# Feed-forward tiles of a two-layer encoder: transposed by DMA in two 16-bit planes instead of on TensorE

## The chip, the cores and the metric

The kernel runs on one core of a Trainium2 chip. The metric is device time of one execution in microseconds. The kernel before was run three times: 2039.32, 2039.69 and 2040.37 us, median 2039.69.

## The reference

Two encoder layers work on 256 tokens of width 2048. Each layer mixes tokens, attends to 256 memory tokens, projects out, and ends in a gated feed-forward of width 5632:

```python
D_FF = ((8 * D_MODEL // 3 + 255) // 256) * 256

def swiglu(h, w_gate_up, w_down):
    gate, up = jnp.split(h @ w_gate_up, 2, axis=-1)
    return (jax.nn.silu(gate) * up) @ w_down

def reference(x, mem, ...):
    for l in range(DEPTH):
...
        x = x + jnp.concatenate([tok_out, mem_out], axis=-1) @ w_out[l]
        x = x + swiglu(rms_norm(x, g_ffn[l]), w_gate_up[l], w_down[l])
    return x
```

All data are float32.

## The kernel before

Every product is made from three products of parts: a matrix is split into a rounded part (`hi`, written as float32r by ScalarE) and the rest (`lo`, subtracted by VectorE), and TensorE multiplies hi by hi, lo by hi and hi by lo (lines 198 to 200 in `matmul3`). For weights the split is `halves` (L254 on ScalarE, L255 on VectorE); for activations it is `split` (L192, L193). SP loads the weights from HBM into `raw` tiles, of which there are four; the split weights `whi` and `wlo` have three buffers each, so ScalarE can run at most two buffers ahead of the one that TensorE reads.

The feed-forward of a layer runs over 11 feature blocks of 512 columns, in chunks of 4, 4 and 3 blocks. For each block a `Pair` multiplies the normalized input (`hF`) by the block's gate and up columns, in eight steps over the 2048 rows of the weights; a step loads a 256-row strip of both. Up to three of the eight steps ("fast") use sums of the operands to save one of eight products: VectorE makes the sums of the weights (L347 to L350, into `raw` and `T`), and both `raw` and `T` are split. The other steps split `raw` alone. Then ScalarE makes silu of the gate (L785), VectorE multiplies by up (L786) into a tile `sg` of 128 tokens by 512 features, one for each of the two row tiles t.

For the down projection the features must lie on the partitions, so `turn_a` transposes each `sg` tile: four TensorE transposes of 128x128 into a PSUM bank (L204, through `transpose4`), then `split` into hi and lo. For some blocks (`quick`) a copy of two of the four pieces (L773, 128x256) is kept in SBUF, from which `activation_sums` makes the sums that fast steps of the down projection need. `turn_a` is called with a delay by `later`: 12 steps after its block, or 3 steps for the last block of a chunk. After a chunk's blocks two Pairs of the down projection add the chunk's share to the residual X.

Calls of `later` and the order of statements give the order of the program; the tile framework's scheduler then interleaves the instructions of each engine. Each engine works through its queue in that fixed order and waits at an instruction whose operands are not there. Feed-forward tiles of 512 columns (`big`) come from a pool of 26 (`FFN_TILES`).

Of the kernel before, what the change touches and what calls it, by code (L numbers as in the profile page):

```python
# [9 lines left out]

F32 = mybir.dt.float32
F32R = mybir.dt.float32r
AF = mybir.ActivationFunctionType
ALU = mybir.AluOpType
AX = mybir.AxisListType

P = 128
# [36 lines left out]
def encoder(ctx: ExitStack, tc: tile.TileContext, x, mem, g_mix, g_ffn, w_in_a, g_v_a, w_spatial, b_spatial,  # L54
            w_in_b, g_q_b, g_k_b, g_mem, w_mem_kv, g_mq, g_mk, w_out, w_gate_up, w_down, rope_c, rope_s, out):
    nc = tc.nc
# [14 lines left out]
    def nm(s):  # L71
        uid[0] += 1
        return f"{s}_{uid[0]}"

    def big(dt=F32, shape=None):
        return room["p"].tile(shape or [P, NB], dt, tag="a", name=nm("a"))
# [4 lines left out]
    def misc():  # L81
        return psm.tile([P, NB], F32, tag="m", name=nm("m"))

    def v4(a):
        return a.rearrange("p (c n) -> p c n", n=P)
# [10 lines left out]
    def later(delay, fn):  # L96
        queue.append((clock[0] + delay, len(queue), fn))
# [24 lines left out]
    def load_x(t, j):  # L122
        nc.sync.dma_start(X[t][j], x[0, t * P:(t + 1) * P, j * NB:(j + 1) * NB])
# [3 lines left out]
    def load_gain(kind, g, tile):  # L127
        gst[kind] = tile
        nc.scalar.dma_start(gst[kind], g.rearrange("l (c p) -> (l c) p", p=P))
# [7 lines left out]
    def gslice(kind, l):  # L137
        return gcol[kind][:, 16 * l:16 * l + 16]

    load_gain("mix", g_mix, kp.tile([32, P], F32, tag="sg", name="gst_mix", bufs=2))  # L140
    nc.scalar.activation(junk[:, :8], mhalf, AF.Square)
    load_x(0, 0)
# [45 lines left out]
    def split(src, shape):  # L188

        hi = big(F32R, shape)  # L190
        lo = big(F32R, shape)
        nc.scalar.copy(hi, src)  # L192
        nc.vector.tensor_tensor(lo, src, hi.bitcast(F32), ALU.subtract)  # L193
        return hi, lo
# [7 lines left out]
    def transpose4(src, dst):  # L202
        for c in range(4):
            nc.tensor.transpose(dst[:, c * P:(c + 1) * P], src[:, c * P:(c + 1) * P], ident)  # L204

    def square_sum(src, out):
        for i in range(2):
            nc.scalar.activation(junk, src[:, 2 * P * i:2 * P * (i + 1)], AF.Square, accum_out=out[:, i:i + 1])

    def norm_piece(src, t, j, g, parts, keep):  # L210

        tp = misc()
        transpose4(src, tp)
        gained(tp, t, j, g, parts, keep)
        return tp
# [4 lines left out]
    def gained(tp, t, j, g, parts, keep):  # L220

        hi = keep(F32R, [P, 4, P])
        lo = keep(F32R, [P, 4, P])
        for c in range(4):
            gc = g[:, 4 * j + c:4 * j + c + 1]
            nc.scalar.activation(hi[:, c, :], v4(tp)[:, c, :], AF.Copy, scale=gc)
            nc.vector.scalar_tensor_tensor(lo[:, c, :], v4(tp)[:, c, :], gc, hi[:, c, :].bitcast(F32), ALU.mult,
# [20 lines left out]
    def halves(raw, n, step=KC4):  # L248

        hi = wp.tile([P, KC4, NB], F32R, tag="whi", name=nm("whi"))[:, :n]  # L250
        lo = wp.tile([P, KC4, NB], F32R, tag="wlo", name=nm("wlo"))[:, :n]
        for c in range(0, n, step):
# [47 lines left out]
    def activation_sums(a0, a1):  # L300

        q = big(F32, [P, 4, P])
        nc.vector.tensor_tensor(q[:, 0], a1[:, 0], a1[:, 1], ALU.subtract)
        nc.vector.tensor_tensor(q[:, 2], a1[:, 0], a0[:, 0], ALU.subtract)
        nc.vector.tensor_tensor(q[:, 1], a0[:, 0], q[:, 0], ALU.subtract)
        nc.vector.tensor_tensor(q[:, 3], a0[:, 1], q[:, 1], ALU.subtract)
        hi, lo = split(q, [P, 4, P])
        return [(hi[:, i, :], lo[:, i, :]) for i in range(4)]
# [106 lines left out]
    def head_norm(acc, r, gain, rope=False):  # L415

        ss = small(8)
        for t in range(NT):
            for h in range(4):
                hs = slice(h * P, (h + 1) * P)  # L420
                nc.scalar.activation(junk[:, :P], acc[t][:, hs], AF.Square, scale=r[t],
                                     accum_out=ss[:, 4 * t + h:4 * t + h + 1])
# [24 lines left out]
    def heads_T(qn):  # L447

        hi = [big(F32R, [P, 2, S]) for _ in range(2)]
        lo = [big(F32R, [P, 2, S]) for _ in range(2)]  # L450
        for t in range(NT):
            ts = slice(t * P, (t + 1) * P)
            tp = misc()
            transpose4(qn[t], tp)
            for pr in range(2):
                src = v4(tp)[:, 2 * pr:2 * pr + 2, :]
                nc.scalar.copy(hi[pr][:, :, ts], src)
                nc.vector.tensor_tensor(lo[pr][:, :, ts], src, hi[pr][:, :, ts].bitcast(F32), ALU.subtract)
        return hi, lo

    def attend(qn, waits, keys, values, kv_of, kc0, parts):
# [10 lines left out]
        def scores(pr):  # L472
            for h in (2 * pr, 2 * pr + 1):
# [10 lines left out]
                for t in range(NT):  # L484
                    nc.scalar.activation(pe[:, t * S:(t + 1) * S], sc[:, t * S:(t + 1) * S], AF.Exp,
                                         bias=nmx[:, t:t + 1], accum_out=sm[:, t:t + 1])
# [40 lines left out]
    def scaled(acc, r):  # L527

        res = []
        for t in range(NT):  # L530
            hi = big(F32R)
            lo = big(F32R)
            nc.scalar.activation(hi, acc[t], AF.Copy, scale=r[t])
            nc.vector.scalar_tensor_tensor(lo, acc[t], r[t], hi.bitcast(F32), ALU.mult, ALU.subtract)
# [64 lines left out]
    def residual_turns(j, norm, g, parts):  # L599
        add_residual(None, j, norm, g, parts)  # L600
# [4 lines left out]
    for l in range(DEPTH):  # L605
# [4 lines left out]
        if l == 0:  # L610
# [15 lines left out]
            def turn_spatial(i, a):  # L626
                tp = misc()
                transpose4(a, tp)
                wsT[i] = big()
                nc.scalar.copy(wsT[i], tp)  # L630
# [80 lines left out]
        else:  # L711
# [12 lines left out]
            for c in range(3):  # L724
                acc = linear(hT, w, c * NB)
                attend(head_norm(acc, norm.r, ghead["q"], True), (5, 6, 10, 13), lambda: own["k"], lambda: own["v"],
                       lambda h, c=c: (4 * c + h) // 3, 4 * c, cat)
# [32 lines left out]
        for chunk in (range(0, 4), range(4, 8), range(8, 11)):  # L760
            aT, aS, half = Parts(), {}, {}
            quick = [2 * f + 1 for f in chunk[:2 if chunk[-1] < 10 else l]]

            def turn_a(a, t, f, aT=aT, aS=aS, half=half, quick=quick):
                tp = misc()
                transpose4(a, tp)
                hi, lo = split(v4(tp), [P, 4, P])
                for i in range(4):
                    aT.put(4 * f + i, t, hi[:, i, :], lo[:, i, :])
                i = 2 * f + 1  # L770
                if i in quick:
                    half[i, t] = big(F32, [P, 2, P])
                    nc.scalar.copy(half[i, t], v4(tp)[:, 2:4])  # L773
                    if t == NT - 1:
                        aS[i] = activation_sums(half[i, 0], half[i, 1])

            pairs = {}
            for f in chunk:
                order, some = ((3, 4, 5, 0, 6, 1, 7, 2), 2) if f == 0 else ((0, 3, 1, 4, 2, 5, 6, 7), 3)
                pairs[f] = Pair(hF, sums, w_gate_up[l], f * NB, DFF + f * NB, order, fast[:some])  # L780
            for f, g in pairs.items():
                g.run(pairs.get(f + 1))
                for t in range(NT):
                    a = kp.tile([P, NB], F32, tag="sg", name=nm("sg"), bufs=2)
                    nc.scalar.activation(a, g.out[t][0], AF.Silu, scale=norm.r[t])  # L785
                    nc.vector.scalar_tensor_tensor(a, g.out[t][1], norm.r[t], a, ALU.mult, ALU.mult)  # L786
                    later(3 + t if f == chunk[-1] else 12 + t, lambda a=a, t=t, f=f: turn_a(a, t, f))
            last = chunk[-1] == 10
            every = [2 * f + c for f in chunk for c in range(2)]
            slow = [i for i in every if i not in quick]  # L790
            pairs = []
            for jj in range(2):
                order = list(slow)
                for n, i in enumerate(quick):
                    order.insert(2 * n + (0 if jj and not last else 2), i)
                into = [[X[t][2 * jj + n] for n in range(2)] for t in range(NT)]
                pairs.append(Pair(aT, aS, w_down[l], 2 * jj * NB, (2 * jj + 1) * NB, order, quick, into))
            for jj, g in enumerate(pairs):
                g.run(None if jj else pairs[1])
                for j in (2 * jj, 2 * jj + 1):  # L800
                    if last and l < DEPTH - 1:
                        residual_turns(j, next_norm, gslice("mix", l + 1), hT)
                    elif last:
                        for t in range(NT):
                            parts = 2 if j == 3 and t == NT - 1 else 1
                            for i in range(parts):
                                cs = slice(i * NB // parts, (i + 1) * NB // parts)
                                eng = nc.scalar if i else nc.sync
                                eng.dma_start(out[0, t * P:(t + 1) * P, j * NB + cs.start:j * NB + cs.stop],
                                              X[t][j][:, cs])  # L810
# [37 lines left out]
```

## Time and profile before

| | |
|---|---|
| median of three runs | 2039.69 us |
| profiled execution, first to last instruction (its span) | 2038.5 us |
| HBM traffic over the span | 194 GB/s |
| TensorE clock granted | 1.000 |
| tiles transposed in the feed-forwards | 44 (176 transposes) |

No separate time of the profiled execution is given beside its span. In the profile PE is TensorE's multiplication, PEld its weight load, DVE is VectorE, ACT ScalarE, POOL GpSimd, SP the engine that issues the weight loads; a q behind the name is an engine's queue of issued DMAs. A row of a group reads: line, engine, operation, output<-input, sizes, count, then busy time in us and mean ns of one, then idle time just before these instructions and what ended most of it. Busy times of one engine overlap somewhat, since instructions are pipelined.

### The profile page before, as it was taken

To read this page: it belongs to the slowest core of one execution; us is meant where nothing else is said; L and a number is where in the kernel's file an instruction comes from. 1 tells how busy PE (TensorE), PEld (TensorE's weight loads), DVE (VectorE), ACT (ScalarE), POOL (GpSimd) and SP (SyncE) were. 2 spreads that over 40 slices of the span, in tenths; PEclk is the share of its full clock that TensorE was granted. 3 is DMA by queue.
4 is the path that set the end of the run, shared out by engine and by line. 5 is a ranking of instruction groups with operands and counts; after the bars stand their busy time and mean duration, and the time that the engine had idled before them with its cause. 6 is when DMAs were issued, how large, how long until landed. Compare 5 with 4: busy or idle time off the path is not lost.

```text
span 2038.5 us, 24693 instructions
## 1 busy us (share of the span) xinstructions
PE 2027.7 (99%) x9298; PEld 1679.9 (82%) x9298; DVE 1605.0 (79%) x1862; ACT 1095.0 (54%) x1389; POOL 50.6 (2%) x80
## 2 busy tenths in 40 slices
PE   9999999999999999999999999999999999999999
PEld 7888888888888888888888888888888888888887
DVE  5675557998879988887566886589979899798876
ACT  7765455454445554444555765555544455444552
POOL 2010000000000000000010100000000000000000
PEclk9999999999999999999999999999999999999999
DMA  9754554646656465665566544555566555565554
GB/s 325 253 179 155 185 188 154 227 165 206 203 190 227 165 207 196 202 227 194 186 198 204 173 133 141 202 185 178 195 206 218 195 184 190 205 221 192 183 197 137
DMA packets 202432, 396.08 MB, mean 194 GB/s; under 512 B 11068, under 2 KB 11432, under 8 KB 202312
## 3 DMA queue, kind: packets, MB, share of 16 engines
q1 hardware_dynamic: 198800, 385.79, 56.6%
q0 software_dynamic: 2048, 6.42, 1.0%
q10 hardware_dynamic: 1464, 2.28, 0.3%
q8 instruction: 73, 1.20, 0.2%
q14 instruction: 47, 0.39, 0.1%
HBM read 390.26 MB, written 4.19 MB: 194 GB/s over the span
## 4 chain that ended last, share of the span: by engine, by line
PE 96%; DVE 3%; DMA 1%; issue 1%; ACT 0%; SPq 0%; DVEq 0%; ACTq 0%
PE acc L200 27%; PE acc L199 27%; PE acc L198 27%; PE m L200 4%; PE m L198 4%; PE m L199 4%; PE m L204 2%; DVE wlo L255 1%; DMA raw<-in_w_gate_up 1%; PE m L500 0%; PE m L643 0%; ACT whi L254 0%; DVE x L413 0%; DVE e L413 0%; DMA x<-in_x 0%
## 5 line engine op out<-in xcount | busy, mean ns | idle before, releaser
L254 ACT CAST whi<-raw 128x2048 fp32r<-128x2048 f32 (+2 forms) x465 | 700.8, 1539 | 585.0 <-PE acc L199 512.5
L255 DVE TENSOR_TENSOR wlo<-raw,whi 128x2048 fp32r<-128x2048 f32 (+2 forms) x465 | 836.4, 1823 | 223.9 <-ACT whi L254 220.1
L198 PE MATMUL acc<-whi,h 128*128 128x512 f32 x1440 | 563.7, 392 | 0.0
L199 PE MATMUL acc<-whi,h 128*128 128x512 f32 x1440 | 562.6, 391 | 0.0
L200 PE MATMUL acc<-wlo,h 128*128 128x512 f32 x1440 | 524.1, 392 | 0.9 <-DVE wlo L255 0.9
L198 PE MATMUL acc<-whi,a 128*128 128x512 f32 x1062 | 414.8, 391 | 0.0
L199 PE MATMUL acc<-whi,a 128*128 128x512 f32 x1062 | 414.2, 390 | 0.0
L200 PE MATMUL acc<-wlo,a 128*128 128x512 f32 x1062 | 398.2, 391 | 0.0
L200 PEld LDWEIGHTS acc<-wlo,h 128*128 128x128 f32 x1440 | 270.6, 188 | 56.6 <-DVE wlo L255 1.5
L199 PEld LDWEIGHTS acc<-whi,h 128*128 128x128 f32 x1440 | 270.7, 188 | 55.3
L198 PEld LDWEIGHTS acc<-whi,h 128*128 128x128 f32 x1440 | 271.0, 188 | 54.0
L200 PEld LDWEIGHTS acc<-wlo,a 128*128 128x128 f32 x1062 | 199.4, 188 | 41.3 <-DVE wlo L255 0.3
L199 PEld LDWEIGHTS acc<-whi,a 128*128 128x128 f32 x1062 | 199.5, 188 | 40.4
L198 PEld LDWEIGHTS acc<-whi,a 128*128 128x128 f32 x1062 | 199.5, 188 | 40.2
L254 ACT CAST whi<-T 128x1536 fp32r<-128x1536 f32 x82 | 121.4, 1480 | 143.8 <-PE acc L199 102.2
L255 DVE TENSOR_TENSOR wlo<-T,whi 128x1536 fp32r<-128x1536 f32 x82 | 143.5, 1750 | 39.1 <-ACT whi L254 39.0
L198 PE MATMUL m<-whi,a 128*128 128x512 f32 x264 | 104.2, 395 | 0.7 <-ACT whi L254 0.7
L199 PE MATMUL m<-whi,a 128*128 128x512 f32 x264 | 102.9, 390 | 0.0
L347 DVE TENSOR_TENSOR raw<-raw 128x512 f32<-128x512 f32 x82 | 56.1, 684 | 54.9 <-DMA raw<-in_w_gate_up 53.5
L200 PE MATMUL m<-wlo,a 128*128 128x512 f32 x264 | 89.6, 389 | 0.0
L192 ACT CAST a<-m 128x512 fp32r<-128x512 f32 x80 | 46.7, 587 | 42.8 <-PE m L204 31.7
L193 DVE TENSOR_TENSOR a<-m,a 128x512 fp32r<-128x512 f32 x80 | 53.8, 682 | 13.1 <-ACT a L192 12.9
(126 smaller groups left out, 1473.1 us busy)
## 6 DMA issues: line engine op xcount, KB each, us to landing
raw<-in_w_gate_up SPq DMA_DIRECT2D x352, 512.0 KB, 4.7
raw<-in_w_down SPq DMA_DIRECT2D x176, 512.0 KB, 5.2
raw<-in_w_out SPq DMA_DIRECT2D x32, 1024.0 KB, 5.1
raw<-in_w_in_a SPq DMA_DIRECT2D x24, 1024.0 KB, 5.2
raw<-in_w_in_b SPq DMA_DIRECT2D x24, 1024.0 KB, 5.1
raw<-in_w_mem_kv SPq DMA_DIRECT2D x16, 1024.0 KB, 5.1
raw<-in_w_in_a SPq DMA_DIRECT2D x7, 512.0 KB, 6.2
x<-in_x SPq DMA_DIRECT2D x8, 256.0 KB, 5.8
```

The lines of the kernel that those rows point to most:

```text
L192: nc.scalar.copy(hi, src)
L193: nc.vector.tensor_tensor(lo, src, hi.bitcast(F32), ALU.subtract)
L198: nc.tensor.matmul(out, lhsT=a[0], rhs=b[0], start=start, stop=False)
L199: nc.tensor.matmul(out, lhsT=a[1], rhs=b[0], start=False, stop=False)
L200: nc.tensor.matmul(out, lhsT=a[0], rhs=b[1], start=False, stop=stop)
L204: nc.tensor.transpose(dst[:, c * P:(c + 1) * P], src[:, c * P:(c + 1) * P], ident)
L254: nc.scalar.copy(hi[:, cut], raw[:, cut])
L255: nc.vector.tensor_tensor(lo[:, cut], raw[:, cut], hi[:, cut].bitcast(F32), ALU.subtract)
L347: nc.vector.tensor_tensor(raw[:, 0], raw[:, 0], raw[:, 1], ALU.add)
```

## The change

A new helper `turned` replaces the four TensorE transposes. It reads a tile of 128x512 float32 as 128x1024 16-bit words. ScalarE copies the words into two planes (all low halves, then all high halves); one DMA transpose of 16-bit words, issued from ScalarE's queue, turns the planes block by block into a second tile; a second ScalarE copy puts the halves together again in the first tile. The values are moved bit by bit, so the result is the same number for number. `turn_a` takes hi and lo from that tile, and the copy of two pieces now stands before the split.

```diff
+U16 = mybir.dt.uint16
...
+    def turned(src):
+
+        a, b = big(F32, [P, 4, P]), big(F32, [P, 4, P])
+        planes = a.bitcast(U16).rearrange("p c n -> p (c n)")
+        nc.scalar.copy(planes.rearrange("p (h n) -> p h n", h=2), src.bitcast(U16).rearrange("p (n h) -> p h n", h=2))
+        nc.scalar.dma_start_transpose(b.bitcast(U16).rearrange("p c n -> p (c n)").rearrange("p (c n) -> p c n", n=P),
+                                      planes)
+        whole = b.bitcast(U16).rearrange("p c n -> p (c n)").rearrange("p (h n) -> p n h", h=2)
+        nc.scalar.copy(planes.rearrange("p (n h) -> p n h", h=2), whole)
+        return a
...
             def turn_a(a, t, f, aT=aT, aS=aS, half=half, quick=quick):
-                tp = misc()
-                transpose4(a, tp)
-                hi, lo = split(v4(tp), [P, 4, P])
-                for i in range(4):
-                    aT.put(4 * f + i, t, hi[:, i, :], lo[:, i, :])
+                whole = turned(a)
                 i = 2 * f + 1
                 if i in quick:
                     half[i, t] = big(F32, [P, 2, P])
-                    nc.scalar.copy(half[i, t], v4(tp)[:, 2:4])
+                    nc.scalar.copy(half[i, t], whole[:, 2:4])
                     if t == NT - 1:
                         aS[i] = activation_sums(half[i, 0], half[i, 1])
+                hi, lo = split(whole, [P, 4, P])
+                for i in range(4):
+                    aT.put(4 * f + i, t, hi[:, i, :], lo[:, i, :])
```

In the changed kernel the lines stand one to twelve further down: the first copy is L211, the DMA transpose L212, the second copy L215, the split L193 and L194, the weight's split L266 and L267, the copy of two pieces L781, silu L796.

The scheduler moves instructions with it. TensorE, first feature block of layer 0, where its first tile was turned; `acc` are PSUM banks, `whi`, `wlo` the split weights, `h` the input's parts. Before:

```order
L198 MATMUL acc_3157<-whi_3352,h_2802 128x512
L204 MATMUL m_3338<-ident,sg_3116 128x128 x4
L199 MATMUL acc_3157<-whi_3352,h_2803 128x512
L200 MATMUL acc_3149<-wlo_3353,h_2771 128x512
L198 MATMUL acc_3149<-whi_3352,h_2771 128x512
```

And now:

```order
L199 MATMUL acc_3157<-whi_3352,h_2802 128x512
L200 MATMUL acc_3157<-whi_3352,h_2803 128x512
L199 MATMUL acc_3191<-whi_3352,h_2802 128x512
L200 MATMUL acc_3191<-whi_3352,h_2803 128x512
L201 MATMUL acc_3149<-wlo_3353,h_2771 128x512
L199 MATMUL acc_3149<-whi_3352,h_2771 128x512
```

The four transposes are gone from between the products, and the first product with the weight's low part stands two products later.

ScalarE, while the third feature block's weights are cast and the second block's two tiles (`sg_3440`, `sg_3443`) are turned. Before, only a cast for the sums of the block ahead stood between the weights:

```order
L254 CAST whi_3529<-T_3488 128x1536
L254 CAST whi_3562<-raw_3522 128x2048
L254 CAST whi_3593<-raw_3554 128x2048
L254 CAST whi_3597<-T_3557 128x1536
L192 CAST a_3384<-a_3379 128x512
L254 CAST whi_3634<-raw_3590 128x2048
```

And now:

```order
L266 CAST whi_3529<-T_3488 128x1536
L211 COPY a_3662<-sg_3440 128x1024
L212 DMA_TRANSPOSE a_3663<-a_3662 128x8x128
L215 COPY a_3662<-a_3663 128x1024
L781 COPY a_3667<-a_3662 128x256
L193 CAST a_3669<-a_3662 128x512
L266 CAST whi_3562<-raw_3522 128x2048
L211 COPY a_3692<-sg_3443 128x1024
L266 CAST whi_3593<-raw_3554 128x2048
L266 CAST whi_3597<-T_3557 128x1536
L212 DMA_TRANSPOSE a_3693<-a_3692 128x8x128
L215 COPY a_3692<-a_3693 128x1024
```

Both tiles' copies back (L215) stand directly behind the transpose that they wait for, ahead of the next weight's cast.

ScalarE at the end of the first chunk, where the fourth block's tiles are turned while the down projection begins. Before:

```order
L254 CAST whi_4168<-raw_4111 128x2048
L785 ACTIVATE sg_4070<-e_3947,s_447_2824 128x512
L254 CAST whi_4172<-T_4114 128x1536
L192 CAST a_4140<-m_4135 128x512
L254 CAST whi_4209<-raw_4165 128x2048
L192 CAST a_4161<-m_4156 128x512
```

And now:

```order
L266 CAST whi_4168<-raw_4111 128x2048
L796 ACTIVATE sg_4070<-e_3947,s_447_2824 128x512
L211 COPY a_4135<-sg_4067 128x1024
L212 DMA_TRANSPOSE a_4136<-a_4135 128x8x128
L215 COPY a_4135<-a_4136 128x1024
L193 CAST a_4140<-a_4135 128x512
L211 COPY a_4156<-sg_4070 128x1024
L266 CAST whi_4172<-T_4114 128x1536
L212 DMA_TRANSPOSE a_4157<-a_4156 128x8x128
L266 CAST whi_4209<-raw_4165 128x2048
L215 COPY a_4156<-a_4157 128x1024
```

The first tile's transpose and its copy back now stand ahead of the cast of the down projection's first T; the second tile's has one cast between.

## The prediction

> **What bounds the kernel now.** I read the page's first part, then its chain, then the two feed-forward stages by windows.
>
> ```profile
> span 2038.5 us, 24693 instructions
> PE 2027.7 (99%) x9298; PEld 1679.9 (82%) x9298; DVE 1605.0 (79%) x1862; ACT 1095.0 (54%) x1389; POOL 50.6 (2%) x80
> ...
> PE 96%; DVE 3%; DMA 1%; issue 1%; ACT 0%; SPq 0%; DVEq 0%; ACTq 0%
> ```
>
> TensorE is busy for 2027.7 of 2038.5 us, and 96% of the chain that ended last is TensorE: a cycle saved on it is a cycle of the run, as long as nothing else becomes late. The profiled span is 2038.5 us; the median of the three runs is 2039.7, 1.2 us lie around the span. I add every term to 2039.7.
>
> Windows of the two feed-forward stretches between the start-up and the last output blocks (columns: length, then busy time and instructions of PE, PEld, DVE, ACT, POOL, then clock, DMA share, GB/s):
>
> ```profile
> 360.00:786.00 426.00, 425.69 (x1905) 350.94 (x1904) 369.90 (x358) 219.02 (x162) 0.00 (x0) 1.00 0.59 199
> 1380.00:1792.00 412.00, 411.70 (x1845) 339.95 (x1844) 357.56 (x343) 212.46 (x157) 0.00 (x0) 1.00 0.59 198
> ```
>
> Here TensorE idles 0.3 us in over 400. VectorE is at 87%, ScalarE at 51%, the DMA engines at 59%. So the change takes work from the engine that is full and gives it to one that is half empty and to DMA engines that are over half full. ScalarE has the time; the question is whether it has it at the right moments, because it works in order and everything that TensorE multiplies goes through its cast (L254).
>
> **What is removed.** 44 tiles (11 feature blocks, 2 row tiles, 2 layers) lose four transposes each.
>
> ```profile
> L204 PE MATMUL m<-ident,sg 128*128 128x128 f32 x176 | 26.3, 272 | 0.0
> ...
> 90.11 1.31 PE m L204 x12
> ...
> 1002.66 0.87 PE m L204 x8
> ```
>
> A record lasts 272 ns, but they overlap. On the chain twelve take 1.31 us and eight take 0.87: 0.109 us each. 176 x 0.109 = **19.2 us** off the path, 0.94%. The PSUM bank that each tile took also goes; TensorE never waits for one in these stretches, so I count nothing for it.
>
> **What is added on ScalarE.** Per tile two copies of 1024 16-bit elements per partition (L211, L215), one DMA transpose issued from ScalarE's queue (L212) and the wait for it. The cast (L193, before L192) and the quarter copies (L781, before L773) stay, now from SBUF.
>
> ```profile
> L254 ACT CAST whi<-raw 128x1024 fp32r<-128x1024 f32 x199 | 199.7, 1050 | 102.4 <-PE acc L199 84.5 <-issue 11.4 <-DMA raw<-in_w_in_a 4.9
> ...
> L192 ACT CAST a<-m 128x512 fp32r<-128x512 f32 x80 | 46.7, 587 | 42.8 <-PE m L204 31.7 <-PE m L200 5.3 <-PE m L500 4.7
> ...
> L397 ACT COPY e<-m 128x512 f32<-128x512 f32 x32 | 18.5, 578 | 0.0
> ...
> L192 ACT CAST a<-a 128x512 fp32r<-128x512 f32 x15 | 9.3, 619 | 1.0 <-DVE a L306 1.0
> ...
> L773 ACT COPY a<-m 128x256 f32<-128x256 f32 x18 | 6.6, 367 | 7.0 <-DVE a L193 7.0
> ```
>
> No row has 16-bit data. By elements a copy is 1.05 us (1024), by bytes 0.58 (512 words). I take 1.05, since the casts above grow with the count of elements. That is 88 x 1.05 = 92 us more on an engine that idles for 943 us; it costs only where ScalarE is late already. VectorE does the same subtractions as before, from SBUF instead of PSUM: 619 against 587 ns on ScalarE for the like change of source, nothing to count.
>
> **The wait.** Let D be the time from the issue of the transpose to the start of the copy behind it. In the changed order of ScalarE's queue, of the 44 transposes 13 have nothing between issue and copy back, 13 have one cast, 16 have two and 2 have four things. With nothing between, the whole queue stands for D, and behind it stand the casts of the weights. How long can it stand? One place, the second feature block: ScalarE first, then VectorE, then TensorE.
>
> ```profile
> 415.34 1.48 ACT L254 CAST whi<-T 128x1536 fp32r<-128x1536 f32 x1
> 420.56 3.73 ACT L254 CAST whi<-raw 128x2048 fp32r<-128x2048 f32 x2 [3.75 <-PE acc L199]
> 424.18 1.49 ACT L254 CAST whi<-T 128x1536 fp32r<-128x1536 f32 x1
> 425.56 0.63 ACT L192 CAST a<-a 128x512 fp32r<-128x512 f32 x1
> 431.67 3.72 ACT L254 CAST whi<-raw 128x2048 fp32r<-128x2048 f32 x2 [5.48 <-PE acc L199]
> ...
> 422.51 4.49 DVE L255 TENSOR_TENSOR wlo<-raw,whi 128x2048 fp32r<-128x2048 f32 x2 [0.25 <-ACT whi L254]
> ...
> 433.88 2.28 DVE L255 TENSOR_TENSOR wlo<-raw,whi 128x2048 fp32r<-128x2048 f32 x1
> ...
> 428.07 0.39 PE L200 MATMUL acc<-wlo,h 128*128 128x512 f32 x1
> ...
> 436.82 0.48 PE L200 MATMUL acc<-wlo,h 128*128 128x512 f32 x1
> ```
>
> The block's first tile is now turned behind the cast that ends at 416.8. ScalarE then idles 3.75 us until TensorE frees a weight buffer; the next cast feeds a subtraction that ends at 422.51 + 2.28 = 424.8, and TensorE first reads it at 428.07, 3.3 us later. So 7.0 us are free there, and the tile puts 1.05 + D + 1.05 + 0.37 + 0.59 into them: TensorE waits once D is over 4.0. The second tile comes behind the cast that ends at 425.7: 6.0 us until the next cast (the small cast at 425.56 moves away), 0.66 us from the end of its subtraction (436.16) to its use (436.82), less 1.05 + 1.05 + 0.37 leaves 4.2. I take 4.0 for the 13 bare places. A cast between hides 1.5 us more (the shorter, 1.48), two hide 3.4 (1.48 and 1.91). So the wait costs
>
> 13 x (D - 4.0) + 13 x (D - 5.5) + 16 x (D - 7.4), each term from zero up.
>
> Behind it in the queue stand the weight casts; behind those VectorE's subtractions, of which the tile's own (L194) now stands ahead of a weight's in places, and then TensorE.
>
> **How long is D?** No transpose by DMA is in the trace. The plain transfers of the same 256 KB:
>
> ```profile
> memT<-a ACTq DMA_DIRECT2D x8, 256.0 KB, 4.8
> a<-memT POOLq DMA_DIRECT2D x8, 256.0 KB, 3.2
> ...
> a<-in_w_spatial POOLq DMA_DIRECT2D x3, 256.0 KB, 9.8
> ```
>
> Out of SBUF from the same queue 4.8 us, into SBUF 3.2, and 9.8 where the pieces are only 512 B. The transpose reads SBUF and writes SBUF, so 3.2 is the low end; its pieces are small (128 columns of two bytes), so 9.8 is the high end. I take **4.3**, a little above the middle of the two plain rows, being nearest to them in size, direction and layout of the source. At 4.3 the wait costs 13 x 0.3 = **3.9 us**; at 3.2 nothing; at 9.8, 75 + 56 + 38 = 169 us.
>
> The Trainium skill weighs in on both sides. "Advanced Engine Details and Errata", X-Bar Transpose (TRN2), says that transpose DMAs are as fast as regular ones; no run here shows it, and by it D is that of the plain rows, 3.2 to 4.8, which is the first case below. "VectorE: DVE Perf Modes", The three transpose paths, gives 1309 ns for one 128x128 block of 16 bits by DMA against 390 ns on TensorE, and advises TensorE where PSUM will do; our tile is eight such blocks, and if they add up, an estimate of 10.5 us for D, it is the last case below, at 2224 us.
>
> **The DMA engines.** 44 x 256 KB is 11.5 MB beside 396 MB, 3%. It hurts only where a weight is awaited.
>
> ```profile
> raw<-in_w_gate_up SPq DMA_DIRECT2D x352, 512.0 KB, 4.7
> ...
> DVE raw L347 <- DMA raw<-in_w_gate_up: 53.5, 19, 5.0
> ```
>
> 19 times, about once per feature block, VectorE waits for a weight at the head of the queue. Two of these (1 MB) take some 4.7 us, so 256 KB beside them add up to 1.2 us. Two transposes are in flight for some 9 to 12 of the 41 us of a block, so three in ten of 22 blocks collide, 22 x 0.3 x 1.2 = 8 us on VectorE; the lead in front of TensorE (0.66 to 3.3 above) covers about half. I take **4 us**, from 0 to 26 (every block, no cover). The transposes also take completion semaphores that SP's weight loads shared among themselves before; a load then waits for an earlier transpose to land. The loads run several buffers ahead, and I price this within the 26. The two extra tiles per turn come from the pool of 26; the planes copy waits for VectorE's or ScalarE's own work only, never for TensorE, so nothing for it.
>
> **Sum.** 2039.7 - 19.2 + 3.9 + 4 = 2028.4, so **2028 us**.
>
> **The rivals.**
> - *Wait covered* (my forecast): D up to 4.85, where the cost is 11 + 4. Time 2019 to 2035.6. For it: the idle times of 3.75 and 5.48 us at the very places, and plain rows of 3.2 and 4.8. Chance 0.45.
> - *The wait eats the gain*: D 4.85 to 5.45; at 5.2, 15.6 + 4 - 19.2 leaves 2040. For it: 4.8 from this same queue, before anything is added for turning. Chance 0.13.
> - *The wait becomes the bound, slower*: ScalarE's queue stands behind a bare transpose while weight casts are due. It decides from D = 5.45 on. At 6.5: 32.5 + 13 + 4 - 19.2 = +30, 2070 us. For it: leads of 0.66 us and VectorE at 87%, which catches up slowly; against it: at two tiles in three a cast stands between. Chance 0.25 for D up to 8 (2044 to 2119).
> - *The transpose runs at the pace of small pieces*, D of 8 to 10: at 9.8, 169 + 4 - 19.2 gives 2194 us. For it the 9.8 us row; against it, that row reads from outside SBUF. Chance 0.17.
> - That transposes stay on TensorE can be excluded: no L204 on an sg tile is left in the changed order.
>
> **How the numbers follow.** A measurement of this kernel can tell about 0.2% (4.1 us) from no change: faster means below 2035.6, slower above 2043.8. Faster 0.45, same 0.13, slower 0.42. The forecast's own range is 2019 to 2035.6. Since cases of both signs hold most of the chance, the range goes from 2019 to 2120 and leaves out the last case (0.17) and little at the low end.
>
> **What would show it.** Right: no L204 on sg; TensorE's busy time some 19 us less; ScalarE's wait for the transpose in front of L215 of at most 2 to 4 us; L254 still idle for PE acc L199 in the main; VectorE's wait for the gate-up weights still near 54 us. Wrong in the wait: the longest waits of ScalarE are for the transposed tile, TensorE's idle time shows wlo or whi behind it in the feed-forward stretches, and L215 starts over 5 us after L212. Wrong in the copies: L211 or L215 over 1.5 us each. Wrong in the DMA term: the weights' time to landing well over 4.7 us, and VectorE's waits for them a multiple of 54 us.

## The result and the profile after

The changed kernel took **2055.21 us** (median of 4 runs, 2051.64 to 2059.12) against 2039.83 of the kernel before (4 runs, 2039.32 to 2040.37): ratio 1.0076, 95% interval 1.0062 to 1.009. It is slower by 15 us, where the prediction said 12 us faster. The profiled execution took 2057.4 us, 1.8 more than its span.

First the page of the changed kernel: its span, the engines' busy times, and the shares of the chain that ended last.

```profile
span 2055.6 us, 24400 instructions
...
PE 2022.1 (98%) x9122; PEld 1665.1 (81%) x9122; DVE 1607.9 (78%) x1862; ACT 1186.5 (58%) x1477; POOL 50.6 (2%) x80
...
PE 88%; DVE 4%; DMA 3%; ACT 3%; issue 2%; SPq 0%; ACTq 0%; DVEq 0%
```

The 176 transposes are gone (9298 to 9122 matmuls), but TensorE's share of the chain fell from 96% to 88%. Span less busy time is its idle time: 33.5 us, where it was 10.8. And its busy time fell by 5.6 us, not 19.2. So the span's +17.1 us is -19.2 for the removed work, +22.7 idle, and +13.6 in which TensorE was busy for the same work longer. The windows of the two feed-forward stretches, with the columns as in the prediction:

```profile
360.00:786.00 426.00, 418.61 (x1824) 341.94 (x1823) 367.89 (x353) 250.92 (x194) 0.00 (x0) 0.99 0.65 208
1380.00:1792.00 412.00, 405.24 (x1764) 330.85 (x1763) 354.44 (x343) 244.25 (x189) 0.00 (x0) 0.99 0.64 206
```

TensorE now idles 7.4 and 6.8 us where it idled 0.3, and the granted clock is 0.99 instead of 1.00. The clock explains most of the longer busy time: the trace's records of it show 0.5 for 6.8 us at 536.7, 796.1 and 1553.8 us, and for 3.4 us at 1813.2. That is 24 us at half speed, about 12 of the 13.6 us.

**Where TensorE waits.** All four half-clock stretches begin at one kind of place, the change from the first to the second Pair of the down projection of a four-block chunk. TensorE's timeline of the changed kernel at the first of them (start, duration, instruction, in brackets the idle time before it and what ended that; lines are those of the changed kernel, in which the matmuls are L199 to L201, the casts L193 and L266, the subtractions L194 and L267):

```profile
532.88 0.73 PE L201 MATMUL m<-wlo,a 128*128 128x512 f32 x2
535.88 0.50 PE L199 MATMUL acc<-whi,a 128*128 128x512 f32 x1 [2.27 <-DVE x L425]
...
537.68 0.79 PE L199 MATMUL acc<-whi,a 128*128 128x512 f32 x1 [0.79 <-DVE x L425]
538.27 0.63 PE L200 MATMUL acc<-whi,a 128*128 128x512 f32 x1
...
540.46 0.79 PE L199 MATMUL m<-whi,a 128*128 128x512 f32 x1 [1.13 <-ACT whi L266]
```

Three stalls in 8 us, and none is for a transposed tile: twice TensorE waits for a PSUM bank (`acc`) that VectorE frees by adding it to the residual (L425), once for a weight cast. From 537.68 on a matmul takes 0.63 us instead of 0.39. The three stalls sum to 4.2 us here and to 3.5, 3.7 and 3.2 at the other three places, 14.6 us of the 22.7. VectorE's timeline of the changed kernel there:

```profile
534.54 0.68 DVE L360 TENSOR_TENSOR T<-raw 128x512 f32<-128x512 f32 x1
535.14 0.68 DVE L425 TENSOR_TENSOR x<-acc,x 128x512 f32<-128x512 f32 x1
535.74 1.28 DVE L417 TENSOR_TENSOR x<-x,e 128x512 f32<-128x512 f32 x2
536.94 0.68 DVE L425 TENSOR_TENSOR x<-acc,x 128x512 f32<-128x512 f32 x1
...
542.57 0.69 DVE L194 TENSOR_TENSOR a<-a,a 128x512 fp32r<-128x512 f32 x1 [0.37 <-PE m L200]
```

The last row is odd: it is the lo part of a feed-forward tile, so of a tile that belongs to the chunk whose down projection is almost over, and what released it is a TensorE product of the second Pair. In the order of the program it reads, with what it waits for (the same row of the kernel before waits for ScalarE's cast alone):

```
L194 TENSOR_TENSOR a_4162<-a_4156,a_4161 128x512 [waits PE_49]
L193 TENSOR_TENSOR a_4162<-m_4156,a_4161 128x512 [waits Activation_49]
```

There are exactly four such rows in the feed-forwards of the changed kernel (the second row tile of the last block of each four-block chunk) and none before. By the order, the tile for lo comes out of the pool of 26 only when the second Pair's first step has used the sums that another tile holds. The products that need this lo then stand behind that step. There are four `acc` banks (the pool `psa`): two stay taken until the products that were moved are done, and the second Pair gets the other two only when VectorE has added them to the residual (the L425 rows at 535.14 and 536.94). So TensorE runs out of banks.

**Where ScalarE waits for the transfer.** The other part is the one that the prediction was about. The waits of the changed kernel (engine, line, for what: us in total, times, longest), then its transposes and their time from issue to landing:

```profile
ACT a L215 <- DMA a<-a: 46.0, 18, 6.1
...
DVE raw L359 <- DMA raw<-in_w_gate_up: 41.0, 15, 4.9
```

```profile
L212 ACTq DMA_TRANSPOSE a<-a x44: 1247/1249/2157, 375.4 to 1998.3; - x44
...
DMA to landing us min/median/max: 3.0/4.3/7.8
```

The median is the 4.3 us that the prediction took for D; the spread from 3.0 to 7.8 is what it left out. At the place that the prediction worked through, ScalarE's timeline of the changed kernel:

```profile
416.13 1.04 ACT L211 COPY a<-sg 128x1024 uint16<-128x1024 uint16 x1
417.20 1.25 ACTq L212 DMA_TRANSPOSE a<-a  x1
421.56 1.17 ACT L215 COPY a<-a 128x1024 uint16<-128x1024 uint16 x1 [4.39 <-DMA a<-a]
...
423.60 1.89 ACT L266 CAST whi<-raw 128x2048 fp32r<-128x2048 f32 x1
425.40 1.04 ACT L211 COPY a<-sg 128x1024 uint16<-128x1024 uint16 x1
426.35 1.90 ACT L266 CAST whi<-raw 128x2048 fp32r<-128x2048 f32 x1
426.47 1.25 ACTq L212 DMA_TRANSPOSE a<-a  x1
428.16 1.48 ACT L266 CAST whi<-T 128x1536 fp32r<-128x1536 f32 x1
429.55 1.18 ACT L215 COPY a<-a 128x1024 uint16<-128x1024 uint16 x1
```

The transfer took 4.36 us, 0.36 over the lead of 4.0 that was worked out, and TensorE stalled at 424.04 for 1.51 us until the weight cast at 423.60 was done. All stalls of this kind (at 424, 428, 1440, 1443, 1524 and 2001) come to 6.3 us in the changed kernel. So by this trace alone the four places where a tile is short weigh more than the wait; whether each would cost that by itself is for the experiments.

### The profile page after: what moved, and what is told of

Its sections match the earlier page's. It is cut to its first block, busy times and chain, and to the rows that moved or that the text cites. A ratio compares the mean times of both kernels' runs of the same rounds, so it can differ in the third digit from the quotient of the medians.

```text
span 2055.6 us, 24400 instructions
## 1 busy us (share of the span) xinstructions
PE 2022.1 (98%) x9122; PEld 1665.1 (81%) x9122; DVE 1607.9 (78%) x1862; ACT 1186.5 (58%) x1477; POOL 50.6 (2%) x80
## 4 chain that ended last, share of the span: by engine, by line
PE 88%; DVE 4%; DMA 3%; ACT 3%; issue 2%; SPq 0%; ACTq 0%; DVEq 0%
PE acc L201 25%; PE acc L200 25%; PE acc L199 25%; PE m L199 4%; PE m L201 4%; PE m L200 4%; DVE wlo L267 2%; ACT whi L266 2%; PE m L205 1%; DMA a<-a 1%; DMA raw<-in_w_gate_up 1%; DMA raw<-in_w_down 1%; PE m L512 0%; DVE x L417 0%; ACT a L211 0%
## 5 line engine op out<-in xcount | busy, mean ns | idle before, releaser
L267 DVE TENSOR_TENSOR wlo<-raw,whi 128x2048 fp32r<-128x2048 f32 (+2 forms) x465 | 837.6, 1823 | 219.6 <-ACT whi L266 216.1
L266 ACT CAST whi<-raw 128x2048 fp32r<-128x2048 f32 (+2 forms) x465 | 702.3, 1539 | 462.9 <-PE acc L200 408.1
L199 PE MATMUL acc<-whi,h 128*128 128x512 f32 x1440 | 563.1, 391 | 2.9 <-ACT whi L266 2.9
L201 PE MATMUL acc<-wlo,h 128*128 128x512 f32 x1440 | 518.8, 391 | 2.1 <-DVE wlo L267 2.1
L199 PE MATMUL acc<-whi,a 128*128 128x512 f32 x1062 | 415.3, 393 | 11.3 <-DVE x L425 9.9
L201 PE MATMUL acc<-wlo,a 128*128 128x512 f32 x1062 | 402.5, 392 | 0.2 <-DVE wlo L267 0.2
L201 PEld LDWEIGHTS acc<-wlo,h 128*128 128x128 f32 x1440 | 270.5, 188 | 59.9 <-DVE wlo L267 4.4
L199 PEld LDWEIGHTS acc<-whi,h 128*128 128x128 f32 x1440 | 270.9, 188 | 58.5 <-ACT whi L266 3.8
L199 PEld LDWEIGHTS acc<-whi,a 128*128 128x128 f32 x1062 | 200.0, 188 | 55.5 <-DVE x L425 13.3
L201 PEld LDWEIGHTS acc<-wlo,a 128*128 128x128 f32 x1062 | 200.3, 189 | 41.6 <-DVE wlo L267 0.6
L266 ACT CAST whi<-T 128x1536 fp32r<-128x1536 f32 x82 | 121.4, 1480 | 133.5 <-PE acc L200 106.0
L267 DVE TENSOR_TENSOR wlo<-T,whi 128x1536 fp32r<-128x1536 f32 x82 | 143.6, 1751 | 18.7 <-ACT whi L266 18.6
L199 PE MATMUL m<-whi,a 128*128 128x512 f32 x264 | 105.8, 401 | 5.7 <-ACT whi L266 5.7
L201 PE MATMUL m<-wlo,a 128*128 128x512 f32 x264 | 91.1, 398 | 0.1
L215 ACT COPY a<-a 128x1024 uint16<-128x1024 uint16 x44 | 51.6, 1174 | 46.2 <-DMA a<-a 46.0
L199 PEld LDWEIGHTS m<-whi,a 128*128 128x128 f32 x264 | 50.5, 191 | 20.3 <-ACT whi L266 10.0
```

Of the source, the lines that this page charges most:

```text
L199: nc.tensor.matmul(out, lhsT=a[0], rhs=b[0], start=start, stop=False)
L201: nc.tensor.matmul(out, lhsT=a[0], rhs=b[1], start=False, stop=stop)
L215: nc.scalar.copy(planes.rearrange("p (n h) -> p n h", h=2), whole)
L266: nc.scalar.copy(hi[:, cut], raw[:, cut])
L267: nc.vector.tensor_tensor(lo[:, cut], raw[:, cut], hi[:, cut].bitcast(F32), ALU.subtract)
```

## The experiments

Two theories. **Pool**: the turn holds one more tile of the pool while the split takes two, the schedule moves products behind the next Pair's first step, and TensorE stalls there. **Wait**: ScalarE's queue stands behind the transfer while weight casts are due. The first four kernels ran beside a kernel before at 2040.75 us (7 runs), the last three beside one at 2040.55 (15 runs); each was run 4 to 10 times.

**The term of 19.2 us by itself (e4_not_turned).** In `turn_a` of the changed kernel, no turn at all:

```diff
-                whole = turned(a)
+                whole = v4(a)
```

> The tiles are not transposed at all: split reads the sg tile as it is, with no TensorE transposes, no copies to planes and no DMA transposes (the down projection then gets untransposed features; the amount of multiplying is unchanged). It measures the removed term by itself. If 176 transposes are worth 0.109 us each on the path: 2039.8 - 19.2 = 2020.6 us, between 2018 and 2023. If the path does not give them back (VectorE or the weights are next in line): near 2030 us or above.

2020.83 us (2020.13 to 2021.23), ratio 0.9904 (0.9887 to 0.992), clock 1.000: 19.9 us less than before. The removed transposes are worth what was worked out, and 2020.8 is about the best that the kernels below can reach.

**A tile given back before the split (e1_back_into_sg).** The second copy writes back into the `sg` tile, so that the planes' tile is free before the split; the transfer and the wait stay.

```diff
-        nc.scalar.copy(planes.rearrange("p (n h) -> p n h", h=2), whole)
-        return a
+        nc.scalar.copy(src.bitcast(U16).rearrange("p (n h) -> p n h", h=2), whole)
+        return v4(src)
```

> The second copy writes the turned words back into the sg tile instead of the first big tile, so that the first big tile is free as soon as the transpose has landed; everything else as in the change. Pool theory (the lo tile of the last turned tile of each four-block chunk waits for TensorE because the pool of 26 is full, which puts four stalls of about 4.2 us and four stretches of 6.8 us at half clock at the turn of the down projection's pairs): all four vanish, 4 x (4.2 + 3.4) = 30 us less than the change, about 2025 us, no L194 in the feed-forward waits for PE, granted clock back to 1.000. Wait theory (ScalarE standing for the DMA transpose makes these casts late): the transposes and their waits are all still there, so the time stays near 2055 us and the half-clock stretches stay.

2050.08 us (2047.47 to 2054.85), ratio 1.0049 (1.0033 to 1.0064), clock 0.996 in the profiled execution. The pool theory, taken as the only cause, missed by 25 us. The four odd rows are gone from the order, and so are the stalls at the four places, but others came: the waits of this kernel and its timelines of ScalarE and TensorE in the second block:

```profile
ACT sg L215 <- DMA a<-a: 57.0, 21, 8.9
```

```profile
426.65 1.47 ACT L266 CAST whi<-T 128x1536 fp32r<-128x1536 f32 x1
428.02 1.04 ACT L211 COPY a<-sg 128x1024 uint16<-128x1024 uint16 x1
429.09 1.25 ACTq L212 DMA_TRANSPOSE a<-a  x1
437.98 1.16 ACT L215 COPY sg<-a 128x1024 uint16<-128x1024 uint16 x1 [8.92 <-DMA a<-a]
439.05 1.89 ACT L266 CAST whi<-raw 128x2048 fp32r<-128x2048 f32 x1
```

```profile
435.60 0.39 PE L201 MATMUL acc<-wlo,h 128*128 128x512 f32 x1
440.99 0.80 PE L199 MATMUL acc<-whi,h 128*128 128x512 f32 x1 [5.00 <-ACT whi L266]
441.59 0.63 PE L200 MATMUL acc<-whi,h 128*128 128x512 f32 x1
```

This is the wait theory's picture. The second tile's transfer is issued with nothing beside it, ScalarE stands 8.9 us for it, and TensorE 5.0 us, to go on at half clock. The same happens in the second layer at 1446 us (4.9 us). In the changed kernel two casts run beside this same tile's transfer (426.35 and 428.16 above) and the copy back need not wait; here both casts stand ahead of the planes copy. With other tiles the scheduler made another order, so this kernel changes more than the pool, and the two causes had to be taken apart by others.

**The shortage without a transfer (e5_pool_only).** In the kernel before, with TensorE's transposes in place, the turned tile is copied from PSUM into a tile that is held through the split, and a second one is held for a short time (a small write and read by GpSimd keep it):

```diff
-                hi, lo = split(v4(tp), [P, 4, P])
+                whole, b = big(F32, [P, 4, P]), big(F32, [P, 4, P])
+                nc.gpsimd.memset(b[:, 0, :8], 0.0)
+                nc.scalar.copy(whole, v4(tp))
+                nc.gpsimd.tensor_tensor(mhalf[:, :1], mhalf[:, :1], b[:, 0, :1], ALU.add)
+                hi, lo = split(whole, [P, 4, P])
```

> The kernel before, transposes on TensorE, no DMA transpose; but the turned tile is copied by ScalarE from PSUM into a big tile and a second big tile is taken for the same time (GpSimd writes 8 columns of it and reads one), so the pool of 26 is as full as in the change. Pool theory: L193 of the last tile of the four-block chunks again waits for TensorE, the four stalls and the half-clock stretches appear without any DMA transpose: 2039.8 + 30 = about 2070 us, 2060 to 2080. Wait theory: nothing waits for a DMA, 44 copies of 0.58 us are hidden on ScalarE, so 2040 us, 2038 to 2043, clock 1.000.

2064.82 us (2064.12 to 2066.65), ratio 1.012 (1.0105 to 1.0135), clock 0.998: 24 us lost with no DMA transpose in the kernel. Its TensorE timeline has the same stalls at the same place:

```profile
537.00 0.50 PE L198 MATMUL acc<-whi,a 128*128 128x512 f32 x1 [1.43 <-DVE x L413]
...
538.80 0.50 PE L198 MATMUL acc<-whi,a 128*128 128x512 f32 x1 [0.84 <-DVE x L413]
...
541.09 0.79 PE L198 MATMUL m<-whi,a 128*128 128x512 f32 x1 [1.32 <-ACT whi L254]
```

This kernel also adds work that the change does not have: GpSimd is busy for 92.2 us instead of 50.6. The first of the four corners below holds the tile without it.

**Both remedies (e2_two_step).** The `sg` tile is written back, and the turn is cut in two: planes and transfer one or two steps earlier than the change has its whole turn, copy back and split two steps after them.

```diff
+            def start_turn(a, t, f, turn_a):
+                b = turn_by_dma(a)
+                later(2, lambda: turn_a(a, t, f, b))
...
-                    later(3 + t if f == chunk[-1] else 12 + t, lambda a=a, t=t, f=f: turn_a(a, t, f))
+                    later(2 + t if f == chunk[-1] else 10 + t, lambda a=a, t=t, f=f, g=turn_a: start_turn(a, t, f, g))
```

> As e1_back_into_sg, and the turn is cut in two: planes and DMA transpose are put one or two steps earlier, the copy back and the split two steps after them, so that in ScalarE's queue 4 instead of 14 transposes have nothing between issue and copy back. Pool theory: the pool may or may not bind again with the tiles live longer; if it does not, what is left is the bare wait: some 7.5 us of stalls seen at three or four places in the change go, about 2020 us, 2019 to 2024. Wait theory: most of the loss goes here and not in e1_back_into_sg, so about 2025 us here against 2055 us there.

**2021.09 us** (2019.14 to 2022.16), ratio 0.9903 (0.9888 to 0.9918), clock 1.000: 19.7 us better than before, within 0.3 us of e4_not_turned. Its page, its transposes, and its windows of the feed-forwards:

```profile
span 2019.0 us, 24435 instructions
...
PE 2006.2 (99%) x9122; PEld 1661.7 (82%) x9122; DVE 1606.2 (80%) x1862; ACT 1184.6 (59%) x1477; POOL 50.4 (2%) x80
```

```profile
L211 ACTq DMA_TRANSPOSE a<-a x44: 1247/1249/2202, 374.4 to 1958.3; - x44
...
  ACT sg L217: 25.9, 10
...
DMA to landing us min/median/max: 3.0/5.0/9.4
```

```profile
360.00:786.00 426.00, 425.72 (x1876) 351.79 (x1875) 379.56 (x370) 254.94 (x196) 0.00 (x0) 1.00 0.67 213
1380.00:1792.00 412.00, 410.64 (x1811) 339.37 (x1810) 364.43 (x352) 242.15 (x186) 0.00 (x0) 1.00 0.66 210
```

The transfers are no faster here (median 5.0, up to 9.4 us), but other work stands beside them: of the 44, 40 have between one and four things between issue and copy back. ScalarE's waits for them fell to 25.9 us in 10, and these reach TensorE hardly anywhere: it idles 0.3 and 1.4 us in the two windows.

**The four corners (f1_no_transfer, f2_no_transfer_sg, f3_two_step_own).** Then each cause alone and none of them. Without a wait: the transfer is replaced by a third copy on ScalarE, so that nothing is turned; once with the changed kernel's tiles, once with the write back into `sg`:

```diff
-        nc.scalar.dma_start_transpose(b.bitcast(U16).rearrange("p c n -> p (c n)").rearrange("p (c n) -> p c n", n=P),
-                                      planes)
+        nc.scalar.copy(b.bitcast(U16).rearrange("p c n -> p (c n)"), planes)
```

> The changed kernel with its two tiles a and b as they are, but the transposing transfer replaced by a third copy on ScalarE from a to b (about 1.0 us instead of the 1.25 us of the issue): nothing is turned (that part is left out), and ScalarE never waits for a transfer. The four splits that wait for TensorE in the schedule are still there. If the shortage of tiles costs by itself what it cost in e5_pool_only (24 us over its base), this is 2020.8 + 24 = 2045 us (2038 to 2052). If the wait for the transfer makes the loss and the shortage only adds to it, it is 2021 (2019 to 2025).

> e1_back_into_sg with the transposing transfer replaced by a third copy on ScalarE from a to b: no wait for a transfer, and no split that waits for TensorE; nothing is turned (that part is left out). If e1's 29 us over the kernel without a turn (2050.1 against 2020.8) are its waits for the transfer, this is 2021 (2019 to 2024). If they are the work added to ScalarE (two copies and an issue for each tile), it stays at 2045 to 2050.

With the changed kernel's tiles 2045.59 us (2043.53 to 2050.35, 10 runs), ratio 1.0026 (1.0017 to 1.0036); with the write back 2018.55 (2018.12 to 2019.11), ratio 0.9892 (0.9875 to 0.9908). The tile that is held costs 27.0 us by itself, and the work added to ScalarE costs nothing that shows. TensorE's timeline of the first of the two, at the first of the four places:

```profile
531.07 0.73 PE L201 MATMUL m<-wlo,a 128*128 128x512 f32 x2 [0.90 <-DVE wlo L266]
533.48 0.50 PE L199 MATMUL acc<-whi,a 128*128 128x512 f32 x1 [1.68 <-DVE x L424]
...
536.48 0.50 PE L199 MATMUL m<-whi,a 128*128 128x512 f32 x1 [1.33 <-ACT whi L265]
```

And the other way round, the turn cut in two but the second copy written into tile `a` as in the change:

```diff
-        nc.scalar.copy(src.bitcast(U16).rearrange("p (n h) -> p n h", h=2), whole)
-        return v4(src)
+        nc.scalar.copy(planes.rearrange("p (n h) -> p n h", h=2), whole)
+        return a
```

> e2_two_step, but the second copy writes back into tile a as in the change, so that two tiles of the pool are taken for each turn again; the turn stays cut in two, with most of the transfer beside other work. Four splits wait for TensorE in the schedule, as in the change. If the shortage acts by itself: about as f1_no_transfer, 2045 us (2038 to 2052). If the wait for the transfer made the loss: 2021 (2019 to 2025).

2050.32 us (2045.06 to 2053.21), ratio 1.0044 (1.0031 to 1.0057), with the groups of stalls at 531, 789, 1544 and 1800 us again. ScalarE's waits for the transfer are as short here as with the write back (25.3 us in 9, where it was 25.9 in 10), and yet the cut in two brings 5 us without it and 29 with it.

The order agrees with the times. The four rows in which a lo part of a feed-forward tile waits for TensorE stand in the change, e5_pool_only, f1_no_transfer and f3_two_step_own, and in none of the other four: the kernel before, e1_back_into_sg, e2_two_step and f2_no_transfer_sg.

| | tile `a` held through the split | written back into `sg` |
|---|---|---|
| one step, transfer | 2055.2 (the change) | 2050.1 |
| two steps, transfer | 2050.3 | 2021.1 |
| one step, no transfer (nothing turned) | 2045.6 | 2018.6 |

These come from three groups of runs, whose kernels before lie within 1 us of each other (2039.8, 2040.8 and 2040.6). Against the corner without either, the pool costs 27.0 us, the wait 31.5, both together 36.7. The 31.5 hold all that the transfer brings in one step; its traffic alone is not it, since the kernel at 2021.1 moves the same 44 tiles. Each alone is more than the gain of 19.2, and taking away one of them leaves most of the loss. Why the two together cost 22 us less than their sum was not tried apart; the orders differ, and in the changed kernel the stalls of the wait are 6.3 us, where e1_back_into_sg has 16.3 in its six largest.

## Why the prediction was wrong, step by step

- **The removed transposes, 19.2 us**: right. 19.9 measured with nothing turned.
- **The copies, 1.05 us each, hidden**: right. 1.04 and 1.17 us in the rows of the changed kernel, 97.5 us together where 92 were estimated; with three copies in place of two the kernel is at 2018.6 us, so they cost no time that shows.

```profile
L215 ACT COPY a<-a 128x1024 uint16<-128x1024 uint16 x44 | 51.6, 1174 | 46.2 <-DMA a<-a 46.0
...
L211 ACT COPY a<-sg 128x1024 uint16<-128x1024 uint16 x44 | 45.9, 1043 | 5.1 <-DVE sg L797 5.0
```

- **The DMA engines, 4 us**: too high, if anything. VectorE's waits for gate-up weights fell from 53.5 to 41.0 us, and the weights' landing from 4.7 to 4.4. If the collisions lengthen a transfer, it is the other one, the transpose (below).
- **The pool, 0 us**: this step failed, and by itself it turns the sign. The prediction said that the two extra tiles come from the pool of 26 and that "the planes copy waits for VectorE's or ScalarE's own work only, never for TensorE, so nothing for it". That is true of the planes copy. But `a` is still held when the split takes two tiles more, and it is the last of these, lo, that gets its place only from TensorE. It costs 27.0 us alone.
- **The wait, 3.9 us**: the mechanism was right, and one place, but the term was mis-sized. Alone it measured 31.5 us. The median D of 4.3 was right; the lead of 4.0 set against it was not. The prediction followed the cast through VectorE's subtraction to TensorE's first read of `wlo`, at 428.07. But TensorE reads the cast itself first. In the kernel before this is the row

```profile
423.76 0.39 PE L198 MATMUL acc<-whi,h 128*128 128x512 f32 x1
```

  which by the order reads `whi_3562`, the first of the two casts at 420.56. That cast took 1.9 us, so the read comes 1.3 us after its end, and not 3.3 us as for `wlo`. By this path the lead at the first tile is 3.75 + 1.3 less the 3.06 of the tile's own copies and cast, so 2.0 us. In the changed kernel it is this read that stalls:

```profile
425.55 0.50 PE L199 MATMUL acc<-whi,h 128*128 128x512 f32 x1 [1.51 <-ACT whi L266]
```

  A transfer of 4.36 us with 1.51 of stall makes a lead of 2.9. Other places have more: for the transfer issued at 973 us ScalarE stood 5.4 us, and no stall of TensorE followed. So one lead and one D for all bare places was wrong in both directions. In e1_back_into_sg it was the long transfers that cost most, 8.9 and 8.7 us of ScalarE's wait with stalls of 5.0 and 4.9 behind them; and a stall also lowered the clock. The counts were off slightly too: in the order 14, 11, 17 and 2 transposes have none, one, two and four things behind them, not 13, 13, 16 and 2.
- **The rivals**: "the wait becomes the bound, slower" came nearest in sign and mechanism, but it asked for D over 5.45, where the median in the changed kernel was 4.3. The wait's own part there was just over a quarter of TensorE's new idle time. That 2055 us lies within this rival's 2044 to 2119 is luck: most of the loss came from the tile that is held, of which it knew nothing.
- **The clock** stood in no term. In the profiled execution of the changed kernel some 12 us of the loss are work at half clock, at the four places whose stalls sum to 3 to 4 us each.

## What to carry to other kernels

A change that takes tiles from a pool is judged at every tile taken while the new one is still held, and the order tells: which instructions wait for another engine now that did not before. A transfer put into the middle of an in-order queue wants its issue and its use cut apart, with work of others between; a median time to landing says little where the cost begins at a threshold, and the lead ends at the first instruction that reads anything from behind the wait. And where two causes each exceed the gain, undoing one shows almost nothing: they are told apart only with the corner that has neither.

## What the runs showed of the hardware

- Short stalls cost twice. In e1_back_into_sg TensorE's granted clock fell to 0.5 for 6.8 us during each of the two long stalls (5.0 and 4.9 us). In the changed kernel it fell for 6.8 us or 3.4 us at the four places, where no single stall is longer than 2.3 us; at the first place it fell after one stall, at the others after the second or during the second or third. The windows of e1_back_into_sg around its stall of 5.0 us (the clock is the third number from the right):

```profile
430.00:435.00 5.00, 5.00 (x24) 4.12 (x23) 1.12 (x1) 0.00 (x0) 0.00 (x0) 1.00 1.13 295
435.00:440.00 5.00, 0.99 (x5) 0.49 (x3) 0.00 (x0) 2.02 (x2) 0.00 (x0) 0.92 0.51 96
440.00:445.00 5.00, 4.01 (x10) 3.14 (x10) 4.03 (x5) 5.00 (x5) 0.00 (x0) 0.50 0.13 18
```

  Not every such group of stalls drew it: in f1_no_transfer the places at 533 and 789 us, whose stalls sum to 4.5 and 4.1 us, kept the full clock, and in f3_two_step_own three of the four did. What decides it stays open. The Trainium skill ("TensorE: Matmul & The Clock Gate", HAM oscillation — how this bites in real kernels) gives the rule of no idle gap over about 3.4 us. The stall of 5.0 us agrees with it; the changed kernel's drop at 536.7 us does not, since the longest single gap before it was 2.27 us. The changed kernel's spread (2051.6 to 2059.1 us) goes with the clock of its runs, 0.998 and 0.997 in the two faster, 0.994 and 0.995 in the two slower.
- An issue of a DMA need not wait for the work ahead of it in its queue. In the order of the changed kernel both casts (426.35 and 428.16 in ScalarE's timeline above) stand ahead of the second transfer's issue, and yet it is recorded at 426.47, as soon as its planes were copied (425.40 + 1.04). In all 44 the issue is recorded within 0.3 us of that copy's end. So the things between the planes copy and the copy back are what covers the transfer, and not only those behind the issue, which the prediction counted: counted so, 8 of the 44 are bare and not 14.
- The DMA transpose of 256 KB in 16-bit words mostly took 1.25 us to issue. From the packets of the changed kernel's trace: with under 0.6 MB of weights moving meanwhile (19 of 44) its last packet was done a median 2.6 us after the issue, with more 4.7 us. The two go together in the records, but a longer transfer also meets more weights, and the weights' traffic was not varied. Of the two pages that the prediction weighed, "Advanced Engine Details and Errata" of the Trainium skill (X-Bar Transpose (TRN2): as fast as regular DMAs) agrees with the median of 4.3 us against 4.8 and 3.2 of the plain transfers in the kernel before; the sum of eight blocks, 10.5 us by the figure of "VectorE: DVE Perf Modes" (The three transpose paths), was not reached by any of the 44.
